# Mirrored rotation tables in the S5 layers, and rounded products for the last twelve gated DeltaNet input tiles

## The chip, the cores and the metric

The kernel runs on one core of a Trainium2 chip, in one launch. The metric is device time in microseconds (us). Five engines matter here and each works through its own queue in order: TensorE (PE; its weight loads are listed as PEld), VectorE (DVE), ScalarE (ACT), GpSimd (POOL) and SyncE (SP), which issues the DMAs. Matmuls write to PSUM, which this kernel handles as eight banks.

## The reference, cut to what matters

The program is one step of a four-layer decoder trunk for 256 prompt tokens and 8 x 4 sample tokens, 288 columns together, with a model width of 1024 in float32. Layers 0 and 3 mix tokens with an S5 layer (a complex diagonal state space and a gated linear unit, GLU), layer 1 with an RG-LRU and layer 2 with a gated DeltaNet. A convolutional feed-forward block follows every mixer. The two parts that the change touches compute this:

```python
# S5: u = x @ w_in; per group a complex diagonal recurrence over time
a_bar = exp(lam * dt)                         # |a_bar| e^{i theta}, one per state
h[t]  = a_bar * h[t-1] + b_bar @ u[t];   y[t] = Re(c @ h[t]) + d * u[t]
out   = val * sigmoid(gate),  (val, gate) = gelu(y) @ w_glu

# gated DeltaNet: proj = x @ w_in gives q, k, v, z (8 heads x 128 columns each) and a, b
q, k, v = silu(conv4(q, k, v));  then the chunked delta rule on q, k, v -> o, state
out = (rmsnorm(o) * silu(z)) @ w_out
```

## The kernel before

Everything is kept transposed, channels on the 128 partitions and the 288 tokens along the row. A product with a weight matrix is a sequence of output tiles of 128 channels; one tile sums k = 0 to 7 (or more) blocks of 128 rows into one PSUM bank. There are two ways to multiply a tile.

- **Three products of rounded parts.** Weight and operand are each cut into a rounded part and the rest, both in the type float32r: `wh` by a copy (line 552, mostly ACT), `wl = w - wh` by a subtraction (line 564, DVE or POOL), and the operand's `xh`, `xl`. Each k takes three matmuls, wh*xh, wh*xl and wl*xh (`part`, line 611).
- **Whole.** The raw weight tile `wr` is multiplied by an unrounded operand in plain float32. The trace lists two matmul records for each k. Nothing is cut.

`whole` (line 512) says which units go whole: the S5 input, the second half of the RG-LRU input, and the gated DeltaNet's input tiles from number `NP3` = 8 on.

**What sets the order.** The whole program is written out by a planner at build time (`Net`). The matrix products are the spine. Between two matmul groups `tick` (line 423) lets every waiting task, a generator, write out its next piece, by rank, once the planner's own estimate of time says that its inputs are there. `ahead` (line 523) issues weight loads, cuts `wh` up to four units ahead of the product in work and `wl` up to three. Weight loads share four raw buffers; a raw buffer of a cut unit is free when `wl` is made, that of a whole unit when its product is done. Once written, each engine runs its list in order and waits only on real semaphores.

**S5 layer (`s5_tables`, `s5`).** The recurrence is done four time steps at a time, so a prompt row has 64 blocks. To make a complex recurrence a real one, the input is turned by the angle of its block, e^{-i n phi}, scanned with the real radius, and turned back with e^{+i n phi}. The tables of these angles are `ee`, 64 entries for each of 32 state columns. They are built by doubling: entries k..2k-1 are entries 0..k-1 times entry k-1, a complex product of four DVE instructions (`cmul`: two products by a broadcast, one difference, one sum). `few` makes the first 16 entries for all 32 columns; `many` makes 16 -> 32 and 32 -> 64 for 8 columns at a time, in four ranges. In layer 0 the tables are built at the start of the kernel, beside the first input products; in layer 3 they are built during the last product of layer 2's feed-forward block. `prep(m)` and `out(m)` make small matrices for each of eight channel tiles, and `chain(m)` runs tile m: `u` = PSUM times the norm, a bounce through DRAM (`scr`, `rr`), a product into a pair of PSUM banks (`pv`), turn, scan, turn back, product, GELU, split into `gh`, `gl`.

Eight banks are in use at first, four named ps and four named px. `doubles` (line 1240) takes the four px banks back when the last tile in them is done, and makes of them one pair of banks for `pv` and two single ones. The input loop starts it before input tile number `DB` = 4. The first `chain` can only do its `pv` product when the pair exists.

**Gated DeltaNet (`gdn`).** Its 32 input tiles come in the order 0-11, 16-19, 12-15, 20-23, 24-31; tiles 0-7 are keys, 8-15 queries, 16-23 values, 24-31 the gate z. Before tile 8 the operand `xl` is given up and its buffer holds the unrounded operand `xf` (`operand`); tiles 8-31 are whole. The delta rule runs beside the products: `prompt(0)`, `prompt(1)` for four heads each, and `sample(0)`, `sample(1)`, whose states of 512 KB per head (`s0`) are loaded from DRAM into four buffers. `sample(1)` can load when `sample(0)` has stored. Each of its loads ends with a `yield` that returns to the planner only when the load before has landed in the planner's time. At the end `gdn_out` starts with two output tiles, which take block k when head k is done.

Of the kernel before, what the change touches and what calls it, by code (L numbers as in the profile page):

```python
# [36 lines left out]
HJ = 2  # L37
OE, CE = 0, 'a'
NK = 4, 10
PRS, DB, TH, BI = 1, 4, 8, 0.0  # L40
SR, SS = (0, 2, 1), (1000.0, 2000.0)
WHOLE = (0, 6)
RB = 1
NP3 = 8
WARM = 3500.0


def ksplit(k):
    n = -(-k // KD)
    e = [k * i // n for i in range(n + 1)]  # L50
    return list(zip(e[:-1], e[1:]))
# [249 lines left out]
class Net:  # L301
# [210 lines left out]
    def whole(self, u):  # L512

        name, m = self.units[u][:2]
        return name.startswith("s5_in") or name == "gdn_in" and m >= NP3 or name == "lru_in" and m >= KL

    def freed(self, u):
        return (self.over if self.whole(u) else self.cutl) > u
# [58 lines left out]
    def gemm(self, name, ms, nk, rh, rl, ready=None):  # L577

        sp = ksplit(nk)
        jobs, out = [], []  # L580
        for m in ms:
            while len(self.banks.free) <= self.spare or not self.banks.ready():
                self.idle()
            bank = self.banks.pop()
            out.append(bank)
            jobs.append([bank[:, :T], 0])
            for ks in sp:
                w = self.take(name, m, ks)
                late = []
                for i, k in enumerate(range(*ks)):  # L590
                    if ready and not ready(k):
                        late.append((i, k))
                    else:
                        self.part(jobs[-1], w, i, k, nk, rh, rl, bank if ready else None)
                        self.over += i == ks[1] - ks[0] - 1 and not late and self.used == self.over + 1
                        self.tick()
                jobs[-1].append((w, late))
        for k in range(nk):
            for bank, job in zip(out, jobs):
                for w, late in job[2:]:  # L600
                    for i, kk in late:
                        if kk == k:
                            while not ready(k):
                                self.idle()
                            self.part(job, w, i, k, nk, rh, rl, bank)
                            self.tick()
        self.over = self.used
        self.fin = self.now
        return out

    def part(self, job, w, i, k, nk, rh, rl, late=None):
        o = slice(i * P, (i + 1) * P)
# [433 lines left out]
    def s5_tables(self, li, es):  # L1046
# [6 lines left out]
        def t(n, k=None):  # L1053
            return c.tile([P, Q] if k is None else [P, Q, k], F32, name=n)
        sc = c.tile([P, 3, Q], F32, name="sc")
        self.load(("ss", li), (sc, f"s5_sc{j}"))
        ee, pp, ff = (c.tile([P, 2, Q, k], F32, name=n) for n, k in (("ee", 64), ("pp", L), ("ff", L)))
        (s.er, s.ei), (s.pr, s.pi), (s.fr, s.fi) = ((z[:, 0], z[:, 1]) for z in (ee, pp, ff))
        s.npi = t("npi", L)
        s.rho4 = t("rho4")  # L1060

        def scalars():
# [78 lines left out]
            def first():  # L1141
                ea, eb = (c.tile([P, 2, Q], F32, name=x) for x in ("ea", "eb"))
                yield from self.cmul(u2, u1, u1, ea, eb)
                yield from self.cmul(ee[:, :, :, 0], u2, u2, ea, eb)
                self.mark(("se", li))

            def powers():
# [20 lines left out]
            yield  # L1168

        def double(q0, q1, k, a, b):  # L1170
            e = ee[:, :, q0:q1, :]
            return self.cmul(
                e[:, :, :, k : 2 * k], e[:, :, :, :k], e[:, :, :, k - 1 : k].to_broadcast([P, 2, q1 - q0, k]), a, b
            )

        def few():
            a, b = (x.rearrange("p i (q k) -> p i q k", q=Q) for x in spare)
            yield from self.after(("se", li))
            for k in (1, 2, 4, 8, 16):
                if k in (1, 4, 16):  # L1180
                    yield from unit(ee[:, :, :, k - 1], a[:, :, :, 0], b[:, 0, :, 0])
                if k < 16:
                    yield from double(0, Q, k, a[:, :, :, :k], b[:, :, :, :k])
            self.mark(("s16", li))

        def many(ranges):
            a, b = (x.rearrange("p i (q k) -> p i q k", q=8) for x in spare)
            yield from self.after(("s16", li))
            for q0 in ranges:
                for k in (16, 32):  # L1190
                    yield from double(q0, q0 + 8, k, a[:, :, :, :k], b[:, :, :, :k])
                self.mark(("sr", li, q0 // 4), ("sr", li, q0 // 4 + 1))

        s.tasks = [hinted(scalars(), V, 3), hinted(few(), V, 3)]
# [3 lines left out]
    def s5(self, li, gi, tables=None):  # L1198
# [7 lines left out]
        with ExitStack() as es:  # L1206
# [305 lines left out]
            for m, ps in enumerate(self.gemm(f"s5_in{j}", range(start), KD, self.xh, self.xl, self.xready(g0))):  # L1512
                job(m, ps)
            for m in range(start, KD):
                if m == DB:
                    extra = doubles()
                    next(extra)
                    self.spawn(extra)
                    self.spare = 2
                while m >= TH and not self.marked(("s2", li, m - TH)):  # L1520
                    self.idle()
                job(m, *self.gemm(f"s5_in{j}", [m], KD, self.xh, self.xl))
# [27 lines left out]
    def gdn(self, gi):  # L1550
# [6 lines left out]
        with ExitStack() as es:  # L1557
# [44 lines left out]
            def f32(t):  # L1602
                return t.bitcast(F32)
# [16 lines left out]
            def operand(xf):  # L1620

                for m in range(KD):
                    A.activation(xf[:, m, :], self.x[:, m, :], AF.Copy, scale=self.gains[:, g0, m : m + 1])
                    self.mark(("xf", m))
                    if m % 2:
                        yield
                self.mark("xf")

            def scalars():
                yield from self.after("gw")  # L1630
# [502 lines left out]
            def sample(hg):  # L2133
# [4 lines left out]
                    yield from self.after(("s0", 0))  # L2138
                for i in range(4):
                    t = yield from s0s.get()  # L2140
                    self.fin = self.dma(t, self.a["gdn_s0"][hg, :, i])
                    s0.append(t)
                    yield
                self.mark(("s0", hg))
                mk = vm.rearrange("p (h c) -> p h c", h=4)
                G.memset(mk, 0.0)
# [129 lines left out]
            def rk(m):  # L2276
                return RK[(0, 0, 1, 3, 2, 4, 5, 5)[m // 4]]
# [3 lines left out]
            for m in tiles[start:]:  # L2281
                if m == NP3:
                    while not self.marked("gx"):
                        self.idle()
                    x2 = self.xs.tile([P, KD, T], F32, name="xf", tag="xl"), None
                    self.spawn(operand(x2[0]), rank=-1)
                ready = (lambda k: self.marked(("xf", k))) if m == NP3 else None
                self.spawn(fns[m // NH](m % NH, *self.gemm("gdn_in", [m], KD, *x2, ready)), rank=rk(m))
                if m == NH - 1:
                    for r in range(4):  # L2290
                        self.spawn(gram(r), rank=RK[0])
                    self.spawn(kscalars(), rank=RK[0])
                    self.spawn(rows(), rank=RK[0])
                    self.spawn(inverse(0), rank=RK[0])
                    self.spawn(inverse(1), rank=RK[0])
                elif m in (19, 23):
                    self.spawn(prompt((m - 19) // 4), rank=RK[6])
# [253 lines left out]
```

## Time and profile before

| | us |
|---|---|
| median of 3 runs | 1536.66 (1536.31 to 1537.96) |
| the profiled execution | 1536.59 |
| its span on the chip | 1534.8 |
| PE busy / DVE busy / ACT busy / POOL busy | 1488.3 / 1287.3 / 831.6 / 323.9 |
| mean granted TensorE clock | 0.988 of full |

The span is the time from the first to the last instruction; the execution's time has 1.8 us more around it. From the times at which the weight matrices are loaded and multiplied, the stages are about: S5 layer 0 to 145 us, its feed-forward and the RG-LRU layer with its feed-forward to 720 us, the gated DeltaNet from 720 to 937 us, its feed-forward to about 1162 us, S5 layer 3 from there to about 1315 us, the last feed-forward to the end. Nearly all instructions carry one source line (the planner's wrapper), so the trace is read by the names of tiles: in "wl<-wr,wh", wl is written and wr and wh are read.

### The profile page before, as it was taken

What the parts mean: (1) busy time and instruction counts of PE and PEld (TensorE: products, weight loads), DVE (VectorE), ACT (ScalarE), POOL (GpSimd) and SP (SyncE); (2) the same over time, 40 slices, a digit from 0 to 9 for tenths busy, and PEclk for the clock granted to TensorE, in tenths of its full rate; (3) what the DMA queues carried; (4) which work ended last, traced back from release to release, by engine and by line L of the source; (5) the groups of instructions that cost most, each with busy time, mean ns of one, the idle gap of its engine ahead of it and who ended that gap; (6) DMA issues with size and microseconds to landing.
All of it is one profiled execution on the core that took longest, in us unless ns stands there. A gap on an engine that the chain in (4) does not pass through costs nothing. (4 is left out here: it accounts for less than half of the span.)

```text
span 1534.8 us, 32907 instructions
## 1 busy us (share of the span) xinstructions
PE 1488.3 (97%) x12620; PEld 1388.8 (90%) x12620; DVE 1287.3 (84%) x2911; ACT 831.6 (54%) x1635; POOL 323.9 (21%) x679
## 2 busy tenths in 40 slices
PE   6889999999999999999999999999998999999997
PEld 5679999999988999999977779999997779999997
DVE  8998799975867899965898777999997897899954
ACT  4575566654674566544644344666544655566632
POOL 1010054510111255400101000455200000255400
PEclk9899999999999999999999999999999999999999
DMA  4423455455424554556322536545544325555562
GB/s 174 116 76 119 164 170 168 165 170 175 164 91 134 196 173 166 159 174 175 135 91 70 191 113 214 177 166 166 165 151 134 113 85 177 171 167 165 157 176 81
DMA packets 84478, 230.07 MB, mean 150 GB/s; under 512 B 19040, under 2 KB 27872, under 8 KB 84320
## 3 DMA queue, kind: packets, MB, share of 16 engines
q1 hardware_dynamic: 84320, 227.96, 46.7%
q8 instruction: 99, 1.62, 0.4%
q14 instruction: 59, 0.48, 0.1%
HBM read 216.94 MB, written 10.99 MB: 149 GB/s over the span
## 5 line engine op out<-in xcount | busy, mean ns | idle before, releaser
L243 DVE TENSOR_TENSOR wl<-wr,wh 128x1024 fp32r<-128x1024 f32 (+2 forms) x346 | 408.1, 1180 | 132.9 <-PE ps L243 36.8
L243 ACT ACTIVATE wh<-wr 128x1024 fp32r<-128x1024 f32 (+2 forms) x346 | 353.2, 1024 | 224.4 <-PE ps L243 80.4
L243 DVE SCALAR_TENSOR_TENSOR cv<-ext,par,cv 128x304 f32<-128x304 f32 (+1 forms) x420 | 256.1, 610 | 10.4 <-ACT cv L243 2.3
L243 PE MATMUL px<-xh,wh 128*128 128x288 f32 (+1 forms) x784 | 232.6, 297 | 0.0
L243 PE MATMUL px<-xl,wh 128*128 128x288 f32 (+1 forms) x784 | 231.2, 295 | 0.0
L243 PE MATMUL px<-xh,wl 128*128 128x288 f32 (+1 forms) x784 | 231.1, 295 | 0.0
L243 PE MATMUL ps<-xh,wh 128*128 128x288 f32 x776 | 230.9, 298 | 0.0
L243 PE MATMUL ps<-xl,wh 128*128 128x288 f32 x776 | 228.9, 295 | 0.0
L243 PE MATMUL ps<-xh,wl 128*128 128x288 f32 x776 | 228.7, 295 | 0.0
L243 POOL TENSOR_TENSOR pr<-cv,cv 128x32 f32<-128x32 f32 (+1 forms) x154 | 164.2, 1086 | 55.3 <-DVE cv L243 52.5
L243 ACT ACTIVATE cv<-ext,par 128x304 f32<-128x304 f32 (+1 forms) x210 | 130.6, 626 | 82.4 <-DVE ext L243 75.6
L243 PE MATMUL ps<-gl,wh 128*128 128x288 f32 x568 | 168.4, 296 | 2.8 <-DVE gl L243 2.7
L243 PE MATMUL ps<-gh,wh 128*128 128x288 f32 x568 | 168.8, 297 | 1.4 <-DVE gh L243 1.2
L243 PE MATMUL ps<-gh,wl 128*128 128x288 f32 x568 | 167.8, 295 | 0.8 <-DVE wl L243 0.8
L243 POOL COPY sto<-ext 128x16 f32<-128x16 f32 (+3 forms) x384 | 101.7, 267 | 302.1 <-DVE ext L243 277.9
L243 PE MATMUL px<-gh,wh 128*128 128x288 f32 x536 | 159.4, 297 | 1.0 <-DVE gh L243 1.0
L243 PE MATMUL px<-gl,wh 128*128 128x288 f32 x536 | 159.4, 297 | 0.0
L243 PE MATMUL px<-gh,wl 128*128 128x288 f32 x536 | 159.1, 297 | 0.3 <-DVE wl L243 0.3
L243 PEld LDWEIGHTS px<-xl,wh 128*128 128x128 f32 (+1 forms) x784 | 146.7, 187 | 0.9
L243 PEld LDWEIGHTS px<-xh,wh 128*128 128x128 f32 (+1 forms) x784 | 146.7, 187 | 0.8
L243 PEld LDWEIGHTS px<-xh,wl 128*128 128x128 f32 (+1 forms) x784 | 146.6, 187 | 0.3
L243 PEld LDWEIGHTS ps<-xh,wh 128*128 128x128 f32 x776 | 145.9, 188 | 0.8
(541 smaller groups left out, 2979.1 us busy)
## 6 DMA issues: line engine op xcount, KB each, us to landing
wr<-ffn_up SPq DMA_DIRECT2D x176, 512.0 KB, 3.5
wr<-ffn_down SPq DMA_DIRECT2D x64, 448.0 KB, 3.3
wr<-s_glu SPq DMA_DIRECT2D x32, 512.0 KB, 3.9
wr<-ffn_down SPq DMA_DIRECT2D x32, 512.0 KB, 3.6
wr<-gdn_in SPq DMA_DIRECT2D x32, 512.0 KB, 3.5
wr<-lru_in SPq DMA_DIRECT2D x20, 512.0 KB, 3.3
wr<-s_in SPq DMA_DIRECT2D x16, 512.0 KB, 4.1
wr<-lru_out SPq DMA_DIRECT2D x16, 320.0 KB, 3.0
```

The source lines that it names most:

```text
L243: return f(*a, **k)
```

## The change

There are four edits.

1. **Mirrored rotations.** The 64-entry table `ee` now holds the angles -31..32 instead of 1..64. The doubling works on its upper half `up` (entries 32-63, angles 1..32) and stops at 32: `many` loses the step 32 -> 64. Entry 31 is set to 1 + 0i by two POOL memsets in `few`. Entries 0-30 are the mirror image, real part copied and imaginary part copied with the sign changed, by two ACT instructions per range that write backwards. Turning to and back by the same table gives the same result with any starting angle.
2. **`DB` by layer.** `doubles` starts before input tile 3 in layer 0; layer 3 keeps 4.
3. **Input tiles 20-31 of the gated DeltaNet in three products.** `whole` now holds for tiles 8 to `NP4`-1 = 19. At tile 20 a task `lower` makes `xl` anew, eight DVE instructions, in the buffer that held `xf`. Tile 20 itself runs through `gemm_upper`: all wh*xh and wl*xh first, then the eight wh*xl, each when its block of `xl` is there. The eleven tiles after it go through `gemm` as tiles 0-7 do.
4. **State loads.** In `sample(1)` the four state loads are written without a `yield` between them.

```diff
-PRS, DB, TH, BI = 1, 4, 8, 0.0
+PRS, DB, TH, BI = 1, (3, 4), 8, 0.0
-NP3 = 8
+NP3, NP4 = 8, 20
...
-        return name.startswith("s5_in") or name == "gdn_in" and m >= NP3 or name == "lru_in" and m >= KL
+        return name.startswith("s5_in") or name == "gdn_in" and NP3 <= m < NP4 or name == "lru_in" and m >= KL
...
+    def gemm_upper(self, name, m, nk, rh, rl, ready):
+
+        while len(self.banks.free) <= self.spare or not self.banks.ready():
+            self.idle()
+        bank = self.banks.pop()
+        (ks,) = ksplit(nk)
+        hi, lo = self.take(name, m, ks)
+        mm, ps = self.pe.matmul, bank[:, :T]
+        for k in range(nk):
+            o = slice(k * P, (k + 1) * P)
+            mm(ps, hi[:, o], rh[:, k, :], start=k == 0, stop=False)
+            mm(ps, lo[:, o], rh[:, k, :], start=False, stop=False)
+            self.tick()
+        for k in range(nk):
+            while not ready(k):
+                self.idle()
+            mm(ps, hi[:, k * P : (k + 1) * P], rl[:, k, :], start=False, stop=k == nk - 1)
+            self.tick()
+        self.over = self.used
+        self.fin = self.now
+        return [bank]
...
+        up = ee[:, :, :, 32:]
...
         def double(q0, q1, k, a, b):
-            e = ee[:, :, q0:q1, :]
+            e = up[:, :, q0:q1, :]
...
         def few():
             a, b = (x.rearrange("p i (q k) -> p i q k", q=Q) for x in spare)
+            self.g.memset(ee[:, 0, :, 31], 1.0)
+            self.g.memset(ee[:, 1, :, 31], 0.0)
...
             for q0 in ranges:
-                for k in (16, 32):
-                    yield from double(q0, q0 + 8, k, a[:, :, :, :k], b[:, :, :, :k])
+                yield from double(q0, q0 + 8, 16, a[:, :, :, :16], b[:, :, :, :16])
+                for i in range(2):
+                    e = ee[:, i, q0 : q0 + 8, :]
+                    self.act.activation(e[:, :, 30::-1], e[:, :, 32:63], AF.Copy, scale=1.0 - 2.0 * i)
+                yield
                 self.mark(("sr", li, q0 // 4), ("sr", li, q0 // 4 + 1))
...
-                if m == DB:
+                if m == DB[j]:
...
+            def lower(xl):
+
+                for m in range(KD):
+                    V.scalar_tensor_tensor(
+                        xl[:, m, :], self.x[:, m, :], self.gains[:, g0, m : m + 1], f32(self.xh[:, m, :]),
+                        op0=ALU.mult, op1=ALU.subtract,
+                    )
+                    self.mark(("xl", m))
+                    if m % 2:
+                        yield
...
                 for i in range(4):
                     t = yield from s0s.get()
-                    self.fin = self.dma(t, self.a["gdn_s0"][hg, :, i])
+                    at = self.dma(t, self.a["gdn_s0"][hg, :, i])
                     s0.append(t)
-                    yield
+                    if not hg:
+                        self.fin = at
+                        yield
+                self.fin = at
...
-                ready = (lambda k: self.marked(("xf", k))) if m == NP3 else None
-                self.spawn(fns[m // NH](m % NH, *self.gemm("gdn_in", [m], KD, *x2, ready)), rank=rk(m))
+                if m == NP4:
+                    x2 = self.xh, self.xs.tile([P, KD, T], F32R, name="xl", tag="xl")
+                    self.spawn(lower(x2[1]), rank=-1)
+                    pss = self.gemm_upper("gdn_in", m, KD, *x2, lambda k: self.marked(("xl", k)))
+                else:
+                    ready = (lambda k: self.marked(("xf", k))) if m == NP3 else None
+                    pss = self.gemm("gdn_in", [m], KD, *x2, ready)
+                self.spawn(fns[m // NH](m % NH, *pss), rank=rk(m))
```

## Rows read from the trace of the kernel before

**Rows 1.** The page's head and part 1: busy us (share) xinstructions by engine.
```profile
span 1534.8 us, 32907 instructions
PE 1488.3 (97%) x12620; PEld 1388.8 (90%) x12620; DVE 1287.3 (84%) x2911; ACT 831.6 (54%) x1635; POOL 323.9 (21%) x679
```
**Rows 2.** Windows of S5 layer 0: A:B length, busy by engine, PEclk, DMA, GB/s.
```profile
20.00:116.00 96.00, 79.17 (x964) 62.20 (x964) 94.77 (x226) 56.59 (x131) 7.03 (x6) 0.91 0.35 100
116.00:131.00 15.00, 14.89 (x347) 12.67 (x347) 11.26 (x25) 4.24 (x13) 0.00 (x0) 1.00 0.01 3
```
**Rows 3.** Windows of the gated DeltaNet, the second half.
```profile
820.00:832.50 12.50, 12.50 (x186) 9.41 (x187) 7.72 (x25) 5.37 (x15) 0.40 (x2) 1.00 0.26 86
832.50:870.40 37.90, 37.90 (x523) 29.65 (x522) 31.89 (x88) 17.84 (x63) 2.00 (x7) 1.00 0.46 156
870.40:920.00 49.60, 49.60 (x380) 36.27 (x378) 34.70 (x95) 18.72 (x56) 4.34 (x7) 1.00 0.40 127
920.00:930.00 10.00, 8.99 (x69) 7.86 (x68) 8.34 (x23) 1.09 (x3) 0.00 (x0) 1.00 0.69 231
```
**Rows 4.** Window at the end of layer 2's feed-forward block.
```profile
1150.00:1160.00 10.00, 9.49 (x72) 9.26 (x71) 9.85 (x20) 2.41 (x5) 0.00 (x0) 1.00 0.52 161
```
**Rows 5.** Tile ee: ns min/median/max, first and last start, forms.
```profile
L243 DVE TENSOR_TENSOR fa<-ee x30: 299/424/1011, 17.6 to 1160.5; 128x256 f32<-128x256 f32 x10, 128x512 f32<-128x512 f32 x10, 128x64 f32<-128x64 f32 x8, 128x128 f32<-128x128 f32 x2
```
**Rows 6.** Timeline of DVE, layer 0: start, us, instruction; one step 32 -> 64.
```profile
43.44 0.69 DVE L243 TENSOR_TENSOR fa<-ee 128x512 f32<-128x512 f32 x1
44.05 0.69 DVE L243 TENSOR_TENSOR fb<-ee 128x512 f32<-128x512 f32 x1
...
47.22 0.75 DVE L243 TENSOR_TENSOR ee<-fa,fb 128x256 f32<-128x256 f32 x2
```
**Rows 7.** Timeline of ACT, layer 0: four copies in SBUF of 256 elements.
```profile
58.91 1.72 ACT L243 ACTIVATE vx<-pa 64x256 f32<-64x256 f32 x4 [2.80 <-DVE pa L243]
```
**Rows 8.** Timeline of PE and DVE around the bank switch in layer 0.
```profile
39.41 0.63 PE L243 MATMUL ps<-ident,wt 128*128 128x128 f32 x4 [4.33 <-DVE u L243]
...
56.35 1.91 PE L243 MATMUL px<-rr,vt 128*128 128x72 f32 x16
...
54.08 0.67 DVE L243 TENSOR_TENSOR u<-px,rstd 128x288 f32<-128x288 f32 x1
```
**Rows 9.** Timeline of PE, gated DeltaNet: one whole input tile, and what follows.
```profile
866.48 4.04 PE L243 MATMUL ps<-xf,wr 128*128 128x288 f32 x16
870.36 2.10 PE L243 MATMUL px<-xf,wr 128*128 128x288 f32 x8
```
**Rows 10.** The chain that ended last: start, us, piece; one tile of three products.
```profile
1338.93 3.17 PE px L243 x24
```
**Rows 11.** Timeline of DVE and ACT, gated DeltaNet: cutting one weight tile.
```profile
909.60 1.23 DVE L243 TENSOR_TENSOR wl<-wr,wh 128x1024 fp32r<-128x1024 f32 x1
...
908.51 1.06 ACT L243 ACTIVATE wh<-wr 128x1024 fp32r<-128x1024 f32 x1 [0.75 <-DMA wr<-gdn_out]
```
**Rows 12.** Tile xl: the DVE instruction that makes it.
```profile
L243 DVE SCALAR_TENSOR_TENSOR xl<-x,gains,xh x48: 499/512/520, 140.8 to 1314.5; 128x288 fp32r<-128x288 f32 x48
```
**Rows 13.** Timeline of the SP queue: first and last state load of sample(1).
```profile
853.02 0.34 SPq L368 DMA_DIRECT2D s<-gdn_s  x1
...
870.93 0.43 SPq L368 DMA_DIRECT2D s<-gdn_s  x1
```
**Rows 14.** Timeline of PE and DVE at the gated DeltaNet's end.
```profile
919.97 0.51 PE L243 MATMUL px<-gh,wh 128*128 128x288 f32 x1
...
924.63 0.49 PE L243 MATMUL ps<-busy 128*128 128x224 f32 x3
...
928.13 0.37 PE L243 MATMUL px<-gh,wh 128*128 128x288 f32 x1 [1.01 <-DVE gh L243]
...
927.76 0.22 DVE L243 CAST gh<-sy 128x128 fp32r<-128x128 f32 x1
```
**Rows 15.** Timeline of PE, layer 2's feed-forward: a wait for a cut weight.
```profile
1153.97 0.40 PE L243 MATMUL ps<-gh,wl 128*128 128x288 f32 x1 [0.51 <-DVE wl L243]
```

More of the change, by code (lines that the diff above doesn't have):

```diff
@@ L1143, in first @@
                 yield from self.cmul(u2, u1, u1, ea, eb)
-                yield from self.cmul(ee[:, :, :, 0], u2, u2, ea, eb)
+                yield from self.cmul(up[:, :, :, 0], u2, u2, ea, eb)
                 self.mark(("se", li))
@@ L1180, in few @@
                 if k in (1, 4, 16):
-                    yield from unit(ee[:, :, :, k - 1], a[:, :, :, 0], b[:, 0, :, 0])
+                    yield from unit(up[:, :, :, k - 1], a[:, :, :, 0], b[:, 0, :, 0])
                 if k < 16:
```

## The prediction

> **What bounds the kernel now.** I read the page first, then windows over each stage, then the timelines of the engines in the stages that the change touches. The page [rows 1] says that PE is busy for 1488.3 of 1534.8 us, DVE for 1287.3. So in most stages PE sets the pace, and a change pays where it takes matmul time away, or in the few stages where PE waits. The windows show two such stages, and the change touches both.
>
> In S5 layer 0, from 20 to 116 us, DVE is busy for 94.77 of 96 us, 98.7%, and PE for 79.17 at a granted clock of 0.91 [rows 2]. DVE bounds this stretch, whatever PE does. From 116 to 131 DVE has 3.7 us of gaps: the last chains wait for each other. In the second half of the gated DeltaNet, from 820 to 920 us, PE is busy for every microsecond of three windows, and DVE for 7.72, 31.89 and 34.70 of 12.5, 37.9 and 49.6 [rows 3]: PE bounds it, with DVE not far behind. From 920 on PE has a hole; it resumes the output product at 928.13 after a wait for DVE's gh, cast from the sample heads' result at 927.76 [rows 14]. At the end of layer 2's feed-forward, where layer 3's tables are built, DVE is busy for 9.85 of 10 us, but PE still for 9.49 [rows 4].
>
> **The change part by part.**
>
> *Mirrored rotations, layer 0.* The step 32 -> 64 goes: for each of four ranges two products of 512 elements and a pair of 256. By start times a product takes 0.61 us, and the pair lasts 0.75 [rows 6], together 1.97. (Of the 10 products fa of that size [rows 5], 8 are this step, four in each layer; the other 2 are in the part that stays.) Less the pair's overlap with its neighbour, 0.08 as the products show it (0.69 long, 0.61 apart), that is 1.9, and 4 x 1.9 = 7.6 us of DVE's list. DVE is at 98.7% with more work queued behind, so nearly all of it should come out of the stage: what is late next is DVE's own next instruction. In its place come eight ACT copies of 248 elements that write backwards. No row shows a backward write. The nearest are four strided copies of 256 elements in 1.72 us, 0.43 each [rows 7]; I take that, 3.4 us. Below it can hardly go; above I allow twice, 7 us. ACT is busy for 56.6 of 96 us [rows 2], so either end is hidden in total. The turn of chain 0 waits for one DVE step, then two ACT copies, about 1 us more than now for the first range alone, and behind the copies on ACT wait its own evacuations of PSUM. The two memsets go to POOL, 7 us busy in 96: nothing.
>
> *DB = 3, layer 0.* The first pv product runs at 56.35 us, just after DVE has read u from a px bank at 54.08 [rows 8]: input tile 3 sat in a px bank, and the pair could not be made before. With the switch before tile 3, no input tile is in px, and the pair and two single banks can exist some 10 us earlier; the input product of tile 3 has to find a free bank instead, and PE already waited 4.33 us for one at 39.41. As DVE is full either way, this moves no DVE work out of the stage. It can fill some of the 3.7 us at the end, since the chains start earlier; or it can cost PE a few us of waiting for banks that DVE's load hides, as PE has 17 us of gaps. I take 0, with -3.7 and +4 as ends.
>
> Layer 0 together: -7.5, between -11 and -3.
>
> *Mirrored rotations, layer 3.* The same 7.6 us of DVE, but PE is the bound. What the trace shows lost there is 0.51 us for one cut weight [rows 15]. I take -0.5, between -1 and +1.
>
> *Twelve tiles in three products.* A whole tile takes 870.36 - 866.48 = 3.88 us [rows 9], a tile of three products 3.17 us [rows 10]. So PE saves 0.71 x 12 = 8.5 us. PE's whole list between 820 and 920 stays otherwise the same.
>
> The price is paid on other engines. Twelve wl at 1.23 us of DVE and twelve wh at 1.06 us of ACT [rows 11], and eight xl at 0.51 us [rows 12]: DVE gets 14.8 + 4.1 = 18.9 us, ACT 12.7. ACT is at 43 of 110 us and takes it. DVE is busy for 82.65 of the 110 us from 820 to 930 [rows 3]; with 18.9 more it is 101.5. So DVE's list alone now needs 101.5 us where PE's needs 101.5 too (110 - 8.5). Two lists that depend on each other step by step don't both run without gaps. At layer 0's 98.7% DVE would need 102.9 us, a gain of 7; at 95%, 106.9, a gain of 3.
>
> A page of the Trainium skill, FP8 and Floating Point Precision, section TensorE Precision Notes, says that a true float32 product makes four passes through the array. With four passes as long as one of the three that replace them, a whole tile would be 32 x 0.132 = 4.2 us and the twelve tiles would save 12.7 us instead of 8.5. The trace does not agree: the whole tile is 3.88 us, 3.67 such passes, so the sum keeps 8.5.
>
> *Tile 20.* xl can only be written when tile 15 has read the last of xf. PE has 16 matmuls (2.1 us) of tile 20 before it needs xl, DVE needs 4.1 us plus what is queued before it. But tile 20 has no lone stretch: of the 523 matmul records from 832.5 to 870.4 [rows 3] its four value tiles are 64, and the delta rule's own products stand between them. I allow 1 us, between 0 and 4. The instructions behind xl on DVE are the delta rule's evacuations, late by up to 4.1 us, and PE waits for them if its other work runs out.
>
> *State loads.* The first load of the second four leaves at 853.02, the last at 870.93, 18 us later [rows 13]. Without the yields all four leave within about 2 us, and sample(1) can begin some 15 us earlier. At its end sit sample(1)'s last DVE instructions, for which PE stands still until 928.13; PE spends 919.97 to 924.63 on output blocks, then 3.5 us on filler (products of busy) and waiting [rows 14]. If sample(1) comes off the end, two heads' blocks more are ready and the last gate tile's chain is late next, about 5 us from its tile's end, against 4.7 us of product to do. So up to 2.8 us of this hole goes. Four loads of 512 KB at once share DMA engines that are 40 to 46% busy [rows 3]; the weight loads beside them are issued a tile ahead.
>
> Gated DeltaNet together: PE's bound allows -8.5 - 2.8 + 1 = -10.3, DVE's at 95% about -3. I take -5.5, nearer to DVE's, because the cuts come on top of a queue that is already 84% full between 832 and 870.
>
> **The sum** against the profiled execution's 1536.59 us (span 1534.8 and 1.8 around it): -7.5 - 0.5 - 5.5 = -13.5, so 1523.1; the median is 0.07 above that execution, so 1523.
>
> **Rivals.**
> 1. *DVE takes the gated DeltaNet's gain.* Its list needs 101.5 us at the least; at 92%, 110, and the stage stays as long as it was. For it: the 18.9 us come where DVE is at 84%. Against: between 870 and 920 it has 15 us of gaps. Layer 0 and 3 remain: 1536.66 - 8.0 = 1528.7.
> 2. *Everything comes out.* Layer 0 gives 11, the DeltaNet 10.3, layer 3 0.5: 1515. For it: PE without a gap from 820 to 920. Against: DVE would have to be at 100%.
> 3. *Layer 0 gives nothing*, because its chains, not DVE's total, set the end: one bank pair for eight chains. Against it: 98.7%. Time 1536.66 - 6.0 = 1530.7.
> 4. *1 and 3 together:* 1536, no change.
> 5. *Slower: DVE's 18.9 us land on the delta rule's path.* The place is DVE's in-order queue from 832 us on. Its 27 us of gaps in 820 to 930 are waits for PE's results; if the cuts can't use them, because they come due in bursts when the delta rule's evacuations do, the stage grows by 18.9 while PE's 8.5 is lost in waiting: 1536.66 + 18.9 - 8.0 = 1547.6. It decides from the point where more than 8.0 of the 18.9 us fall on the path. For it: xl stands first in rank at 832. Against: the cuts of wl run up to three tiles ahead, 9.5 us of PE work.
>
> **How the numbers follow.** Forecast 0.50, rival 1 0.16, rival 2 0.09, rival 3 0.10, rival 4 0.08, rival 5 0.07. A measurement of this kernel tells no less than about 0.2%, 3 us, from no change. The forecast's own range is 1517 to 1528; rivals 1, 2 and 3 lie at 1528.7, 1515 and 1530.7, which carries it to 1513 and 1533, with 0.15 outside. Faster by over 0.2% (below 1533.6) are the forecast and rivals 1 to 3: 0.85; within 0.2% is rival 4: 0.08; slower is rival 5: 0.07.
>
> **What would show it.** Right: the window from 20 us to the last chain's gl (126.9 before) ends 6 to 9 us earlier with DVE still above 97%; ACT shows eight ee<-ee copies near 0.43 us in each S5 layer; the first pv product stands near 45 us; tiles 20-31 show 24 records of xh, xl, wl each in 3.17 us when undisturbed; the second four state loads leave within 2 us; PE's hole at the end of the DeltaNet is under 1.5 us. Wrong: backward copies of 1 us and more that hold up ACT's evacuations; PE waiting for wl or for banks between 832 and 920 for more than 5 us in sum; DVE below 90% there while PE has gaps, which would mean a chain of waits and not a full list.

## The result and the profile after

The changed kernel takes 1519.72 us in the median of four runs (1516.83 to 1521.8), the kernel before 1536.49 in four runs beside it (1535.13 to 1537.96). The ratio is 0.989, with a 95% interval of 0.9876 to 0.9903: 16.8 us faster. 1523.0 was forecast, 1513 to 1533 the range. The profiled execution after took 1519.82 us, its span 1518.0.

The first lines of the profile's page, against [rows 1]:

```profile
span 1518.0 us, 33165 instructions
PE 1480.5 (98%) x12725; PEld 1393.6 (92%) x12725; DVE 1278.1 (84%) x2867; ACT 860.3 (57%) x1707; POOL 340.4 (22%) x695
```

PE lost 7.8 us of busy time and DVE 9.2, ACT gained 28.7. To see where the 16.8 us between the two profiled executions went, I lined up the DMA loads and stores that both have. The load with which a stage's successor begins stands earlier by: 6.7 us after S5 layer 0 (the first feed-forward's history, 176.65 to 169.98), 9.1 at the gated DeltaNet's start (720.76 to 711.68), 14.3 after it (951.55 to 937.30); the span ends 16.8 us earlier. So layer 0 gave 6.7, the DeltaNet 5.2. The other 4.9 stand in stretches whose code the change does not touch (2.4 before the DeltaNet) or that it touches in layer 3 only (2.5 behind it).

**S5 layer 0.** Windows of the kernel after, against [rows 2]; columns as there.

```profile
20.00:116.00 96.00, 87.74 (x1137) 70.77 (x1136) 92.56 (x218) 61.13 (x150) 14.49 (x12) 0.93 0.35 100
116.00:131.00 15.00, 14.74 (x244) 13.41 (x233) 11.24 (x19) 7.21 (x11) 0.00 (x0) 1.00 0.24 68
```

The table `ee` of the kernel after, by operation (ns least/median/most, first and last start), against [rows 5]:

```profile
L243 DVE TENSOR_TENSOR fa<-ee x22: 301/418/1020, 17.6 to 1135.7; 128x256 f32<-128x256 f32 x10, 128x64 f32<-128x64 f32 x8, 128x128 f32<-128x128 f32 x2, 128x512 f32<-128x512 f32 x2
L243 ACT ACTIVATE ee<-ee x16: 392/410/412, 43.6 to 1137.1; 128x248 f32<-128x248 f32 x16
```

Timeline of PE and DVE after: the first and the last rotation product (`pv`), and the last chain's `gl`:

```profile
47.10 3.60 PE L243 MATMUL px<-rr,vt 128*128 128x72 f32 x16 [1.03 <-DMA rr<-scr]
...
106.88 2.00 PE L243 MATMUL px<-sx,vt 128*128 128x72 f32 x16
...
122.76 0.46 DVE L243 TENSOR_TENSOR gl<-g,gh 128x288 fp32r<-128x288 f32 x1
```

Eight of the ten 512-element products `fa` are gone; eight copies for each layer stand in their place, at 0.41 us each. The first `pv` product came forward from 56.35 to 47.10 [rows 8]. DVE, at 98.7% before, now has 3.4 us of gaps in the 96. The last `gl` came forward by 7.3 us: it was at 130.05 before. (The 126.9 that the prediction named is the last but one.)

**Gated DeltaNet.** Windows after, against [rows 3]:

```profile
820.00:857.00 37.00, 36.92 (x597) 31.86 (x598) 32.82 (x82) 23.70 (x63) 2.83 (x9) 1.00 0.40 142
857.00:904.00 47.00, 47.00 (x464) 43.06 (x463) 37.69 (x91) 31.07 (x93) 10.65 (x15) 1.00 0.44 143
904.00:915.00 11.00, 9.28 (x66) 6.57 (x65) 10.55 (x38) 2.67 (x9) 1.42 (x2) 1.00 0.29 78
```

Up to 904 PE has next to no gap, and DVE is busy for 70.5 of 84 us: 84%, with the 18.9 us of new work taken in. The second four state loads leave together:

```profile
852.48 1.91 SPq L368 DMA_DIRECT2D s<-gdn_s  x4
```

PE's hole at the end did not close but grew, from 3.5 us [rows 14] to 9.8 (903.93 to 913.77). In it 3.4 us are filler and 1.7 idle; the rest is the last heads' own transpositions, small products and state updates. The chain that leads to it, from the timeline of PE, DVE and ACT after; between the first line and the fifth lie the 24 products of input tile 28, in 3.17 us:

```profile
883.18 0.30 PE L243 MATMUL px<-xh,wh 128*128 128x288 f32 x1
883.38 2.12 DVE L243 TENSOR_TENSOR wl<-wr,wh 128x1024 fp32r<-128x1024 f32 x1 [3.83 <-PE px L243]
885.42 0.68 DVE L243 TENSOR_TENSOR vt<-vt,fh 128x512 f32<-128x512 f32 x1
886.02 0.45 DVE L243 TENSOR_TENSOR z<-px,rstd 128x288 f32<-128x288 f32 x1
886.35 0.29 PE L243 MATMUL ps<-xh,wh 128*128 128x288 f32 x1
887.38 0.43 ACT L243 ACTIVATE z<-z 128x288 f32<-128x288 f32 x1
887.84 0.23 ACT L243 ACTIVATE vsm<-z 128x32 f32<-128x32 f32 x1
888.87 0.27 PE L243 MATMUL px<-ident,st 128*128 128x128 f32 x1
889.18 0.37 ACT L243 ACTIVATE st<-px,pk 128x128 f32<-128x128 f32 x1
891.91 0.34 DVE L243 SCALAR_TENSOR_TENSOR vts<-px,pk,vts 128x128 f32<-128x128 f32 x1
...
900.76 0.29 PE L243 MATMUL px<-gh,wh 128*128 128x288 f32 x1
...
913.49 0.22 DVE L243 CAST gh<-sy 128x128 fp32r<-128x128 f32 x1
913.77 0.40 PE L243 MATMUL px<-gh,wh 128*128 128x288 f32 x1 [0.21 <-DVE gh L243]
```

And the same chain in the kernel before:

```profile
896.23 4.15 PE L243 MATMUL px<-xf,wr 128*128 128x288 f32 x16
900.51 0.45 DVE L243 TENSOR_TENSOR z<-px,rstd 128x288 f32<-128x288 f32 x1
900.74 0.76 ACT L243 ACTIVATE z<-z 128x288 f32<-128x288 f32 x2
901.20 1.26 DVE L243 COPY vsm<-z 128x32 f32<-128x32 f32 x2 [0.25 <-ACT z L243]
902.59 0.27 PE L243 MATMUL px<-ident,st 128*128 128x128 f32 x1
902.90 0.37 ACT L243 ACTIVATE st<-px,pk 128x128 f32<-128x128 f32 x1 [1.40 <-PE px L243]
905.85 0.34 DVE L243 SCALAR_TENSOR_TENSOR vts<-px,pk,vts 128x128 f32<-128x128 f32 x1
```

Read it from the top. Tile 27 is the last gate tile of heads 0 to 3; its `z` is made at 886.02. In the code (`output`) the transposition of the first sample heads' result (`ident,st`) is written behind a step that waits for these gates. It does not read them: the next instruction, `sy`, does. So its place is the planner's, and PE comes to it in the order of its list without a wait. There is one buffer `st` for a group's working values, and that transposition is its last reader: 0.3 us later the second sample heads write their first `st`, and everything that they still have to do, three solve steps, output, normalisation, follows. 24.3 us later comes their `gh`, and PE resumes. PE had begun the output product at 900.76, 10.1 us earlier after the stage's start than before [rows 14] (8.5 of it are the twelve tiles at 0.71), and then ran out of finished heads. Only 5.3 of the 10.1 remain at 913.77.

### The profile page after: what moved, and what is told of

Its sections match the earlier page's. It is cut to its first block, busy times and chain, and to the rows that moved or that the text cites. A ratio compares the mean times of both kernels' runs of the same rounds, so it can differ in the third digit from the quotient of the medians.

```text
span 1518.0 us, 33165 instructions
## 1 busy us (share of the span) xinstructions
PE 1480.5 (98%) x12725; PEld 1393.6 (92%) x12725; DVE 1278.1 (84%) x2867; ACT 860.3 (57%) x1707; POOL 340.4 (22%) x695
## 5 line engine op out<-in xcount | busy, mean ns | idle before, releaser
L243 PE MATMUL ps<-xh,wh 128*128 128x288 f32 (+1 forms) x832 | 249.6, 300 | 0.0
L243 PE MATMUL ps<-xh,wl 128*128 128x288 f32 (+1 forms) x832 | 245.2, 295 | 0.0
L243 PE MATMUL px<-xh,wh 128*128 128x288 f32 x824 | 245.1, 297 | 0.0
L243 PE MATMUL ps<-xl,wh 128*128 128x288 f32 (+1 forms) x832 | 245.0, 295 | 0.0
L243 PE MATMUL px<-xl,wh 128*128 128x288 f32 x824 | 243.0, 295 | 0.0
L243 PE MATMUL px<-xh,wl 128*128 128x288 f32 x824 | 242.8, 295 | 0.0
L243 PEld LDWEIGHTS ps<-xh,wh 128*128 128x128 f32 (+1 forms) x832 | 155.7, 187 | 3.3 <-issue 1.8
L243 PEld LDWEIGHTS ps<-xl,wh 128*128 128x128 f32 (+1 forms) x832 | 155.4, 187 | 2.1 <-issue 0.8
L243 PEld LDWEIGHTS px<-xh,wh 128*128 128x128 f32 x824 | 154.9, 188 | 1.5 <-issue 1.0
L243 PEld LDWEIGHTS ps<-xh,wl 128*128 128x128 f32 (+1 forms) x832 | 155.6, 187 | 0.3
```

The lines of the kernel that those rows point to most:

```text
L243: return f(*a, **k)
```

## Experiments

The twelve kernels were all timed beside the kernel before. "After the stage's start" counts from the load of `wab`, at 720.76 us before and 711.68 after.

**e1: mirrored rotations alone** (edits 2, 3 and 4 undone).

```diff
-PRS, DB, TH, BI = 1, (3, 4), 8, 0.0
+PRS, DB, TH, BI = 1, (4, 4), 8, 0.0
-NP3, NP4 = 8, 20
+NP3, NP4 = 8, 99
...
```

> The kernel before with the mirrored rotations alone, in both S5 layers (pair switch before tile 4, whole tiles 20 to 31 and the paced state loads as before). The theory on record, DVE's full list bounds S5 layer 0: it gives that layer's 7 us and layer 3's 0.5 to 2, so 1527 to 1530, and the first rotation product (pv) stays near 56 us. Rival, the first pv's late start bounds the layer (47.1 us in the changed kernel, 56.35 before, moved by the switch before tile 3): mirroring alone gives at most 3 us in all, 1533 to 1536, and the 7 us are DB's.

1531.08 us, ratio 0.9967 (0.9954 to 0.9979): the total between the two theories. In its profile layer 0 gives 2.3 us, not 7; 3.5 more come between there and the DeltaNet, where the code is the old one. A window of e1 in layer 0, and its timeline:

```profile
40.00:60.00 20.00, 12.46 (x91) 9.86 (x91) 16.85 (x44) 12.74 (x32) 0.00 (x0) 0.74 0.48 118
```

```profile
54.53 2.55 PE L243 MATMUL px<-rr,vt 128*128 128x72 f32 x16
...
116.82 2.00 PE L243 MATMUL px<-sx,vt 128*128 128x72 f32 x16
...
118.86 1.29 DVE L243 TENSOR_TENSOR x<-px,ee 128x512 f32<-128x512 f32 x2 [3.81 <-PE px L243]
```

The last rotation product of the kernel before:

```profile
114.85 2.00 PE L243 MATMUL px<-sx,vt 128*128 128x72 f32 x16
```

The first `pv` hardly moved, and DVE, with its list 7.6 us shorter, now has 3.2 us of gaps from 40 to 60. The last `pv` stands 2 us later than before, and DVE waits 3.8 us for it. With the early switch it stands 8 us earlier, at 106.88. So the rival had hold of something: the chains, which take turns at one pair of banks, bound the layer as soon as DVE's list is shorter.

**e2: the bank switch before tile 3 alone** (edits 1, 3 and 4 undone).

```diff
-PRS, DB, TH, BI = 1, 4, 8, 0.0
+PRS, DB, TH, BI = 1, (3, 4), 8, 0.0
```

> The kernel before with the bank switch before tile 3 in layer 0 alone. The theory on record (DVE's list is as long as before): within 1.5 us of 1536.5, while the first pv stands near 47 us. Rival (the chains' start bounds the layer): 1530 to 1533. Third: the two need each other, neither alone gives over 2 us, and together they gave 6.7 by the end of layer 0.

1536.74 us in 11 runs, ratio 0.9999 (0.999 to 1.0008): nothing, as the theory on record had it, with `pv` at 48.70. Its profiled execution is the longest of the eleven, 1539.45, and loses 6.8 us in layer 0; from 70 us on PE's granted clock falls there:

```profile
70.00:80.00 10.00, 6.96 (x74) 5.92 (x72) 10.00 (x19) 7.92 (x17) 0.00 (x0) 0.83 0.79 236
80.00:90.00 10.00, 8.37 (x152) 6.66 (x148) 10.00 (x23) 7.65 (x19) 5.64 (x4) 0.72 0.25 58
90.00:100.00 10.00, 10.00 (x106) 9.22 (x99) 9.27 (x19) 5.87 (x17) 1.36 (x1) 0.50 0.05 15
```

By the granted share (an estimate: the length of a stretch times the part of the clock that was withheld) PE loses 13.7 us in layer 0 here and 8.5 in the profile of the kernel before. The other ten runs of e2 have a mean clock of 0.990 to 0.994, this one 0.986, so its profile is not typical of them, and how much of the 6.8 every run loses stays open. Together the two edits gave 6.7, apart 2.3 and nothing. By the end of layer 0 all nine kernels with both are 6.0 to 6.9 us ahead, and e3 and e5, with neither, 0.1 and 0.2 behind: e1's expectation of the theory on record (7 us from the mirrored table alone) failed, and the third reading of e2, that they need each other, holds.

**e3: three products alone** (edits 1, 2 and 4 undone).

```diff
-NP3 = 8
+NP3, NP4 = 8, 20
...
```

> The kernel before with the gated DeltaNet's tiles 20 to 31 in three products alone, state loads paced as before. Theory A, the delta rule's chain through the second prompt and sample heads ends the stage now, and early loads start it: without them the gain falls from the 5.2 us of the changed kernel to 0 to 2.5, 1534 to 1537. Theory B, PE's list ends the stage: 5 to 8 us, 1528.5 to 1531.5. Theory C, DVE's 18.9 us on the chain: slower, above 1538.

1534.08 us in 11 runs, ratio 0.9986 (0.9977 to 0.9995): theory A. The stage is 1.9 us shorter. In the same profile 1.8 us are gained ahead of the DeltaNet, where all its instructions and their order are those of before; that execution is 2.9 us below the median of e3's eleven.

**e4: the changed kernel with paced loads.**

```diff
-                    if not hg:
-                        self.fin = at
-                        yield
-                self.fin = at
+                    self.fin = at
+                    yield
```

> The changed kernel with the second four state loads paced again, as before. Theory A (the sample heads' chain ends the stage, and their loads stand at its head): 2.5 to 5 us longer than the changed kernel, 1522.5 to 1525. Theory A', the chain is set by the second prompt's result and DVE's order behind it, not by the loads: within 1.5 us of 1519.7, and PE's hole before gdn_out's last blocks is as it was (some 10 us with filler).

1523.02 us, ratio 0.9914 (0.9898 to 0.993), 3.3 over the changed kernel: theory A. Here the transposition is early, and the first `st` of the second heads follows the last of their state products instead:

```profile
880.50 0.33 PE L243 MATMUL px<-ident,st 128*128 128x128 f32 x1
...
892.65 0.65 PE L243 MATMUL ps<-s,vm 128*32 128x128 f32 x16
893.42 0.37 ACT L243 ACTIVATE st<-ps,pk 128x128 f32<-128x128 f32 x1 [3.45 <-PE ps L243]
```

So the edit changes the order too: the transposition stands 7.0 us earlier after the stage's start than in the changed kernel, and the last state product 14.1 later.

**e5: early loads alone** (edits 1, 2 and 3 undone).

> The kernel before with the second four state loads unpaced alone. By the prediction's own bound, up to 2.8 us of PE's hole at the gated DeltaNet's end goes: 1533.7 to 1536.5. Theory A (the loads are worth 3.3 us in the changed kernel, because there the sample heads' chain ends the stage and PE has time to spare) says less here, where PE's input products are 10 us longer: 0 to 1.5 us, 1535 to 1536.5. Rival, the loads' gain has nothing to do with the three products: 2.5 to 3.5 us, 1533 to 1534.

1536.78 us in 11 runs, ratio 1.0005 (0.9995 to 1.0015): nothing, theory A's range to 0.3 us. In the kernel before, what the second heads wait for is the first heads' transposition (902.59, above), and the state products were done at 896 without early loads.

**e6 and e7: fewer tiles in three products.**

```diff
-NP3, NP4 = 8, 20
+NP3, NP4 = 8, 24
```

> The changed kernel with tiles 24 to 31 alone in three products; 20 to 23 stay whole, and the new xl stands before tile 24. PE's list grows by 4 x 0.71 = 2.8 us, DVE's falls by four wl, 4.9 us, ACT's by 4.2. Theory A (the chain of prompt and sample heads sets the end, PE has 10 us of hole and filler): 1516 to 1520.5. Theory B (PE's list sets it): 1522 to 1523.5.

> The changed kernel with tiles 28 to 31 alone in three products. PE's list grows by 8 x 0.71 = 5.7 us, DVE's falls by 9.8, ACT's by 8.5. Theory A: the hole before gdn_out's last blocks takes the 5.7 us of PE, 1515 to 1521. Theory B: 1524.5 to 1526.

(e7: 28 in place of 24.) e6 1526.63 us, 0.9935 (0.9922 to 0.9949); e7 1534.43, 0.9983 (0.9975 to 0.9992). Both theories missed: four tiles cost 6.9 us, eight 14.7, two to three times their 0.71 each. PE's waits in e7 between 800 and 960 us:

```profile
PE px L243 <- DVE xl L243: 3.3, 2, 2.5
PE ps L243 <- DVE gh L243: 2.5, 1, 2.5
```

The handover from `xf` to `xl` drains at tile 28, where no product of the delta rule stands beside it; at tile 20 PE waits for no `xl` at all. And the second heads' first `st` comes later, and the clock has a share: see the table below.

**e8: no `wl` for tiles 20 to 31**.

```diff
+        if u < min(self.cuth, self.over + 3) and self.hat[u] <= self.now and self.units[u][0] == "gdn_in" and self.units[u][1] >= NP4:
+            self.raw.pop(u)
+            self.wl[u], self.lat[u] = self.wh[u], self.hat[u]
+            self.cutl += 1
```

> The changed kernel in which tiles 20 to 31 have no wl made: their third product takes wh for it (the low part of these weights is left out), so PE's and ACT's work is as in the changed kernel and DVE's is 14.8 us shorter. If the twelve wl on DVE hold up the prompt's and sample heads' chain: 1512 to 1516.5, with the chain's last gh cast 3 to 5 us earlier and PE's hole at the end of the stage gone. If the chain's length is its own (products, solves and their latencies): 1518.5 to 1520.5, hole as it was.

1519.84 us, ratio 0.9894 (0.9881 to 0.9908), that of the changed kernel: leaving the twelve `wl` out is worth nothing. But the planner gave DVE other work in their place. In the 104 us that end 1 to 2 us behind the last `gh` cast, first of the changed kernel, then of e8 (columns as in [rows 2]):

```profile
811.00:915.00 104.00, 102.19 (x1222) 88.06 (x1221) 87.81 (x229) 62.94 (x178) 15.29 (x28) 1.00 0.42 140
809.70:913.70 104.00, 101.19 (x1238) 86.42 (x1239) 81.93 (x230) 52.11 (x138) 14.82 (x33) 1.00 0.42 136
```

DVE has 5.9 us less to do, not 14.8, and ACT 10.8 less, against the expectation's "as in the changed kernel". So the run shows that 5.9 us less on DVE gain nothing; what 14.8 would do it does not show. The chain is as it was, the transposition 178.1 us after the stage's start against 177.2:

```profile
888.53 0.27 PE L243 MATMUL px<-ident,st 128*128 128x128 f32 x1
888.84 0.37 ACT L243 ACTIVATE st<-ps,pk 128x128 f32<-128x128 f32 x1 [2.15 <-PE px L243]
```

**e9, e10 and e12: the second sample heads' order.**

```diff
             def update(hg, s0, vb):
+                if hg:
+                    yield from self.after(("gs", 1))
...
-            self.spawn(sample(1), rank=RK[7])
+            self.spawn(sample(1), rank=RK[3])
```

> The changed kernel in which the state update of the second sample heads (its products of vm and kts, and their adds onto s on DVE) waits until these heads' gh is written. Theory A, the sample heads' chain ends the stage: four adds of 0.60 us, 2.4 us, leave DVE's queue ahead of the last gh cast, so it comes 2 to 2.4 us earlier after the stage's start than the changed kernel's 202; PE gets the update's products, 1.4 to 2.9 us, out of its hole into gdn_out; together 1518 to 1521. Theory B, PE's list or the gates of the last tiles end it: the cast's place does not move PE, and the 1.4 to 2.9 us are added, 1521 to 1523.

> The changed kernel with the second sample heads ranked as the prompt heads instead of behind them. Theory A: their three solve steps no longer stand behind the prompt heads' normalisation on DVE (5.5 us from first to last st in the changed kernel, 3.5 before), so the last gh cast comes 2 us earlier or more; the prompt heads' last gate product, 2 us ahead of it now, comes next: 1517.5 to 1519. Theory B, what the sample heads win the prompt heads lose: 1519.5 to 1523.

> Both edits of the sample heads together, the rank and the held update. Theory A: they take different things off the same chain, 2 us of solve steps and 2.4 of adds, less the update's 1.4 to 2.9 us of PE: 1516 to 1519, below the changed kernel. Theory B: 1520 to 1525.

e9 (the first edit) 1521.19 us, 0.9906 (0.9892 to 0.992); e10 (the second) 1525.91, 0.9937 (0.9925 to 0.995); e12 (both) 1522.67, 0.9917 (0.9903 to 0.9931). None beats the changed kernel. In e9 the last `gh` comes 1.3 us earlier, not 2 to 2.4, and the update's products behind it cost 2.6. e10 goes theory B's way and past its range: the first heads' transposition is 2.2 us later, and PE takes the second heads' `gh` 3.8 later. e12 lies in theory B's range.

**e11: tiles 12 to 15 as well.**

```diff
-NP3, NP4 = 8, 20
+NP3, NP4 = 8, 12
...
-        return name.startswith("s5_in") or name == "gdn_in" and NP3 <= m < NP4 or name == "lru_in" and m >= KL
+        return name.startswith("s5_in") or name == "gdn_in" and (NP3 <= m < NP4 or 16 <= m < 20) or name == "lru_in" and m >= KL
```

> The changed kernel with tiles 12 to 15 in three products as well (sixteen tiles; in the order written, 12 to 15 stand right ahead of 20 to 31), so the new xl stands four tiles earlier. PE's list 2.8 us shorter, DVE's 4.9 longer, ACT's 4.2. Theory A, the chain ends the stage and its start hangs on where the handover from xf to xl stands: later handovers cost 5.4 us (tile 24) and 7.9 more (tile 28) of stage, so an earlier one gives 1 to 4 us, 1516 to 1519. Theory C, DVE is full where it would stand (17.3 and 18.9 of 20 us busy from 800 to 840): 1521 to 1526. Theory B, PE's tile time alone counts: 1517.

1533.33 us in 11 runs, 0.998 (0.9971 to 0.9989), slower than all three expected. Eight of the runs lie at 1532.8 to 1533.8, three at 1528.0 to 1529.4; the profile is of the fastest. PE waits for `xl` here too (total, times, longest, between 790 and 840):

```profile
PE ps L243 <- DVE xl L243: 5.1, 3, 4.1
```

The longest of these waits lasts from 798.25 to 802.36, and within it the granted clock falls to the lower level. From 800 to 820 us, first e11, then the changed kernel:

```profile
800.00:820.00 20.00, 15.11 (x292) 10.98 (x295) 17.74 (x42) 8.13 (x20) 1.69 (x7) 0.57 0.18 54
800.00:820.00 20.00, 18.88 (x318) 12.80 (x316) 17.25 (x42) 10.86 (x28) 2.28 (x8) 1.00 0.40 133
```

By the granted share e11 loses 8.5 us in the stage, which is 10.4 us longer than the changed kernel's. So it does not tell what an earlier handover is worth at the full clock.

**One table for the stage**, worked out from the profiles, one execution each, in us after the stage's start (the last column to the load with which the feed-forward begins):

| | input done | first `st` of second heads | PE takes their `gh` | stage |
|---|---|---|---|---|
| before | 199.2 | 182.1 | 207.4 | 230.8 |
| after | 189.1 | 177.5 | 202.1 | 225.6 |
| e3 three products | 188.9 | 183.2 | 205.4 | 228.9 |
| e4 after, paced loads | 188.8 | 183.1 | 204.8 | 228.2 |
| e5 loads | 199.6 | 183.9 | 209.5 | 233.0 |
| e6 from tile 24 | 193.8 | 183.1 | 207.1 | 231.0 |
| e7 from tile 28 | 203.0 | 187.5 | 213.8 | 238.9 |
| e8 no `wl` | 190.6 | 178.4 | 202.4 | 226.0 |
| e9 update held | 189.1 | 177.5 | 201.4 | 227.5 |
| e10 sample first | 192.3 | 179.7 | 205.9 | 229.5 |
| e11 from tile 12 | 200.0 | 184.6 | 212.7 | 236.0 |
| e12 both | 192.3 | 179.7 | 203.2 | 231.0 |

The stage ends 23.3 to 23.9 us after PE takes the last heads' `gh` in nine of the twelve; e9 and e12 have the held update in between (26.1 and 27.8), e12 with a clock of 0.66 from 910 to 920, and e7 a clock of 0.91 from 920 to 940 (25.1). From the first `st` to PE's taking of `gh` it is 21.7 to 28.1 us, so the first `st` alone does not give the stage: in e3 it stands 1.1 us later than before, and PE takes `gh` 2.0 us earlier. The shortest, 21.7 and 22.2 in e4 and e3, are those in which the input product ends 5.7 us behind the first `st`; in before, e5, e7 and e11, where it goes on for 15.4 to 17.1 us, they are 25.3 to 28.1. So the length of PE's list seems to be part of this chain; no run tests that by itself. By the granted share the clock takes nothing from the stage in before, after, e4, e5 and e8, 1.7 us in e6, e9 and e10, 3.4 in e3, e7 and e12 and 8.5 in e11, so differences of a few us between these groups are not all order. The end of the input product says little: after, e3 and e4 agree in it to 0.3 us and differ by 3.3 in the stage. In nine kernels the first `st` stands 0.3 us behind the first heads' transposition, in e3 and e4 behind the last state product, in e6 1.9 us behind the transposition.

## Why the prediction was right, and where it was not

*Layer 0, -7.5.* 6.7 by the next stage's load, 7.3 by the last `gl`: right in size, and the copies at 0.41 were taken at 0.43. But two terms have to be put otherwise. The mirrored table alone was worth 2.3 there, since "nearly all of it should come out" counted DVE's list only and not what feeds it; and the bank switch, taken at 0 "as DVE is full either way", is worth 4.4 once DVE is not full. Alone it is worth nothing, as forecast. In e1 what DVE lacked was the last chain's turn at the bank pair. DVE fell to 96.4%, just below the 97% named.

*Layer 3, -0.5.* e1 shows none: its lead changes there by 0.15 us. The 1.5 that the profile after gains in that stage e3 gains too (1.3), without the edit. By the granted share the clock takes 3.4 us there before, 1.7 after and none in e3.

*Gated DeltaNet, -5.5.* 5.2 came. The size was right by luck, the working failed: it weighed PE's list against DVE's, and neither list alone set the end. By its own sign for that (DVE below 90% while PE has gaps) it was a chain of waits. Step by step: 3.17 us for a tile held, as did no wait for `xl` at tile 20 (1 taken, 0 to 4). So did the four loads within 2 us (1.91). A hole of PE under 1.5 us failed: it is 9.8 us. The loads were named as what could take sample(1) off the end, 0 to 2.8 us (by the prediction's own numbers, 3.5 of filler and waiting less 5 - 4.7, it would be 3.2); they are worth 3.3, but only together with the three products (e5, e4), because only then is the state product the later of the two things that the first `st` needs. And the saving of tiles 28 to 31, 2.8 us, lies behind the transposition in PE's list; whether it is worth anything no run tests.

The step that stood for DVE, "nearer to DVE's, because the cuts come on top of a queue that is already 84% full", found no support: e8 takes the `wl` away and gains nothing, though DVE is relieved of 5.9 us only. A cut can hold the queue: the one at 883.38 waited 3.83 us for PE, took 2.12, and tile 27's gate stood behind it. But that did not set the end: in e8 this cut is gone, and the transposition comes no earlier. The GPSIMD Engine Reference of the Trainium skill, section Specifications, says that GpSimd shares its SBUF interfaces with VectorE and contends with VectorE instructions that have two SBUF inputs, among others. The trace agrees: undisturbed this subtraction takes 1.23 us [rows 11], and POOL was scaling states with 128x1024 products then:

```profile
880.66 3.75 POOL L243 TENSOR_TENSOR s<-s,egs 128x1024 f32<-128x1024 f32 x2 [10.54 <-PE px L243]
```

The Trainium skill's Perfetto Trace Analysis, section Identifying the Most-Contended Engine, says to optimise the engine with the highest occupancy first, but on TensorE it calls the busy share of matmuls no good measure and has headroom judged by that of the weight loads or by the share of peak FLOPs. Here PE was at 100% for the 100 us of [rows 3], its weight loads at 75% and DVE at 74%, so by the weight loads PE stood out no more than DVE. PE's input products ended 10.1 us earlier, and 5.2 came out.

*The sum.* 13.5 was forecast, the two stages gave 11.9. The other 4.9 of the 16.8 were not foreseen and are only in part explained. The clock has a share: in the RG-LRU layer of the kernel before

```profile
470.00:480.00 10.00, 7.09 (x39) 5.77 (x38) 8.80 (x28) 3.69 (x7) 1.38 (x2) 0.87 0.61 195
480.00:490.00 10.00, 10.00 (x64) 10.00 (x62) 5.21 (x10) 4.43 (x9) 0.00 (x0) 0.79 0.41 109
```

and of the kernel after

```profile
470.00:480.00 10.00, 9.93 (x63) 9.79 (x64) 5.46 (x11) 4.71 (x9) 0.00 (x0) 0.83 0.46 134
480.00:490.00 10.00, 10.00 (x78) 10.00 (x77) 7.11 (x13) 5.36 (x10) 0.00 (x0) 1.00 0.59 166
```

In three of these four rows PE has for part of the time the lower of its two levels, 1.2 GHz. By the granted share 1.3 + 2.1 us were lost before, 1.7 after; e3, with the same instructions there as before, also gained 1.8. Behind the DeltaNet, in S5 layer 3, it is 3.4 and 1.7 again, so the clock may account for 3.4 of the 4.9. It is not the luck of one execution alone: the mean clock is 0.986 to 0.990 in the 21 runs of before and 0.991 to 0.993 in the four of after. Why it is granted more no run shows. How the rest divides between the newly written order of later stages and differences between executions (the 21 runs of before beside e1 to e4 span 4.6 us) stays open.

What was not tried is the direct test of the chain: a second `st` buffer. Nor was the transposition moved ahead of the wait for the gates, which it does not read. That it is the buffer, and not the order in which the planner wrote the second heads' work, is read from the twelve profiles and not shown by a run that removes it.

## What to carry to other kernels

Where two engines look full, look for the last wait of the stage and follow it back to a buffer or a gate: in nine of twelve kernels this stage ended 23.3 to 23.9 us after PE could take one small cast, and that cast stands at the end of a chain that neither engine's busy share shows. Part of the time saved on a busy engine can turn into waiting there: here 10.1 us became 5.2. Look at the granted clock of each stage before two executions are compared. An edit that is worth nothing alone can be half the gain of another, so price them together.

## What the runs showed of the hardware

The copy that writes 248 elements backwards takes 0.41 us on ACT, no more than a forward copy with a stride, 0.43 for 256 on 64 partitions [rows 7]. A subtraction of 1.23 us on DVE took 2.12 beside a scaling of states on POOL. In e2 PE's granted clock was 0.83 and 0.72 in two windows of 10 us in which PE was busy for 6.96 and 8.37, and 0.50 in the next, in which it was busy for all 10. In e11 it was 0.57 from 800 to 820 us, behind a wait of PE from 798.25 to 802.36. In the kernel before it was 0.52 from 40 to 50 us, where PE was busy for 5.88 and DVE, the bound there, for 9.86 of the 10.
